# Summing the block products of a projection pair in three PSUM banks that are read between products

## The chip, the core and the metric

The kernel runs on one core of one Trainium2 chip. The metric is the device time of one execution in microseconds (us). An execution that the hardware profiler recorded is what the rows below come from. Engines go by the profile's names: PE (matmuls), PEld (weight loads, beside PE), DVE, ACT, POOL, and SP, whose queue issues the transfers.

## The reference, cut to what matters

One layer of a hybrid decoder trunk: 2048 tokens of 1024 channels are normalised, projected by one large matrix, sent through four mixers (RG-LRU, mLSTM, HGRN2, GLA), merged by gates, projected once more and normalised.

```python
def hybrid_mixer(h, w_in, ...):
    u = jnp.einsum('bsd,de->bse', h, w_in).astype(jnp.float32)
    (lru_x, lru_z, m_x, m_o, m_z, h_q, h_f, h_i, h_z,
     g_q, g_k, g_v, g_lr, g_z, merge) = jnp.split(u, idx, axis=-1)
...
    xa = causal_conv(lru_x, lru_conv_w, lru_conv_b)
    y_a = rg_lru(xa, lru_wa, lru_ba, lru_wx, lru_bx, lru_lambda) * jax.nn.silu(lru_z)
...
    gates = jax.nn.sigmoid(merge.reshape(B, S, N_BRANCH, D_MODEL))
    merged = jnp.sum(gates * proj, axis=2)
    return merged @ w_out
```

The change touches only the first line, the product `h @ w_in`, for the columns that are computed channel-major.

## The kernel before, in words

The tokens are worked on in two halves of 1024. In each half `ahead_pairs` (L459) computes 33 pairs of 128-column tiles of the projection with `ip_pair` (L400); then come the mixers and the merge, which the change leaves as they are.

A pair is a product of two blocks of tokens by two blocks of channels on one side, and two blocks of channels by two tiles of columns on the other. Eight block products would do it; `ip_pair` uses seven, in Winograd's form. The token side is split once per half (`split_first`, `split_blocks`: blocks `a11`, `a12`, `a22` and sums `s1` to `s4`). The weight side is made per pair: DVE forms four differences (`wsum`, L427) of the four loaded blocks `b11`, `b12`, `b22` (in the tiles `wr`) and `b21` (in a tile `gth`). For each product `product` (L411) splits its weight block in two float32r parts, the upper on ACT (L416, into a tile `wh`) and the rest on POOL (L417, into `wl`); there are six such buffers. Then PE runs 12 matmuls of 128x512 (L422): four channel blocks by three combinations of parts.

Each product has a PSUM bank of its own, the next of all eight in turn (`bank8`). The names `pb` and `mx` are those banks. The four result blocks are put together in SBUF: ACT copies the first product into `c11` (L437), and seven additions on DVE (`add`, L431) do the rest, each reading one bank and one or two SBUF blocks. `fin` then uses the pair: most take a tanh (L218) and a product (L477) or go to DRAM; those of `lru` run the RG-LRU of one channel tile, with convolutions (L704, L706), small matmuls (L735) and scans (L748) on DVE; those of `mx` run another convolution.

`GORD` (L42) fixes in which order pairs are written: one LRU pair, two path pairs, four times over, then the other paths and the gate pairs. What runs when on each engine is set by the scheduler of the framework, which orders all instructions by priorities and its own clock when the kernel is built. On the chip each engine takes its own queue in that fixed order.

Of the kernel before, what the change touches and what calls it, by code (L numbers as in the profile page):

```python
# [17 lines left out]
HT = 1024  # tokens of a half  # L18
DM = 1024
KT = 8  # k tiles of d_model  # L20
U = 516  # columns of one arena unit
NU = 16  # arena units that stay
NA = 4  # tiles of two units that are the arena's outside of the fast products
NY = 8  # the same, and branch outputs in the merge
NP = 6  # merge gates (of 32) computed between the mixers
NE = 5  # of these, so many for the first tokens while the others are split
EPS = 1e-6
NPB = 2  # PSUM banks of the input projection; the other ones are the mixers'
NG = 10  # arena units of the fast products; the other ones are what follows them
PRE = (("mx", 4), ("mo", 4), ("mz", 4), ("hq", 4), ("hz", 4), ("gz", 4), ("gq", 2), ("gk", 2))  # paths to DRAM, with their tiles  # L30
# [12 lines left out]
NORM = {"hz": "hnw", "gz": "gnw"}  # gate paths with the norm's weight in them  # L43
SILU = ("lz", "mz", "hq", "hz", "gz")
FILL = [0, 2, 0, 0, 0, 1, 0, 0, 1, 0, 0, 0, 2, 0]  # merge gates projected before each stage of the mixers

# columns of the packed per-channel vectors
# [10 lines left out]
# channel-major column tiles of the input projection, in the order of wc  # L58
# [10 lines left out]
# constants that depend on shapes alone  # L69
# [29 lines left out]
class Arena:  # L99
    """Units of U columns, handed out in program order, round and round; pairs start at even units."""  # L100
# [47 lines left out]
class Trunk:  # L148
# [107 lines left out]
    def proj_ch(self, pieces, rh, rl, sink, ns=(0, 1)):  # L256
        """128 columns of a product for 512 tokens at a time from weight pieces of 4 k tiles
        each: sink(token slice, PSUM [128, 512])."""
        nc = self.nc
# [22 lines left out]
    def ip_tok(self, pieces, ncol, evac, single=8):  # L282
        """Token-major column group: evac(first chunk, PSUM [128 tokens, chunks, ncol]); chunks one by one from some."""
        c0 = 0
        while c0 < 8:
            per = 512 // ncol if c0 < single else 1
            v = self.pbank()[:, 0:per * ncol].rearrange("p (c n) -> p c n", n=ncol)
            for cc in range(per):
                for k in range(KT):
                    self.tok_mm(v[:, cc, :], c0 + cc, k, pieces, ncol, k == 0, k == KT - 1)  # L290
            evac(c0, v)
            c0 += per

    def ip_tok_k(self, pieces, evac, ks):
        """The same for 256 columns, k outermost: the operands' tiles are done with one by one."""
# [13 lines left out]
    def split_first(self, xs):  # L309
        """The normalised input of the first tokens"""  # L310
# [7 lines left out]
    def load_first(self, xs):  # L318
        """The first tokens, and merge gates from them before the norm's factor is known"""
# [40 lines left out]
    def split_blocks(self, xs, st):  # L360
        """The other blocks (two of tokens by two of channels) that the products take: one more as it
        is, four sums; the block left out goes to DRAM."""
# [22 lines left out]
    def restore_block(self):  # L385
        """The block left out of the products, where its sum was."""
# [13 lines left out]
    def ip_pair(self, t0, t1, fin):  # L400
        """Two column tiles of 1024 tokens each; fin of both, [128, 3 free + 1024]."""
# [9 lines left out]
        def product(x, w):  # L411
# [6 lines left out]
            ps = self.bank8()  # L418
            for k, (xh, xl) in enumerate(self.op[x]):
                ws = slice(k * 128, (k + 1) * 128)  # L420
                for i, (wp, xp) in enumerate(((hi, xh), (hi, xl), (lo, xh))):
                    nc.tensor.matmul(ps, wp[:, ws], xp, start=(k == 0 and i == 0), stop=(k == 3 and i == 2))  # L422
            return ps
# [5 lines left out]
        def add(o, x, y):  # L429
            with self.prio(self.EV):  # L430
                V.tensor_tensor(o, x, y, op=ALU.add)  # L431
# [3 lines left out]
        p = product("a11", b11)  # L435
        with self.prio(self.EV):
            A.activation(c11, p, AF.Copy)  # L437
        wsum(b11, b12, b11)
        wsum(w2, b22, b11)
        p = product("s2", w2)  # L440
        add(c21, c11, p)
        p = product("s1", b11)
        add(c12, c21, p)
        wsum(b12, b22, b12)
        p = product("s4", b22)
        q = product("s3", b12)
        add(c22, c12, q)
        add(c21, c21, q)
        add(c12, c12, p)
        p = product("a12", b21)  # L450
        add(c11, c11, p)
        wsum(b21, b21, w2)
        p = product("a22", b21)
        add(c21, c21, p)
# [3 lines left out]
    def ahead_pairs(self):  # L458
        """The projections that the mixers take channel by channel, as far as no other channel or  # L459
        earlier token is needed, the RG-LRU, and merge gates: to DRAM."""  # L460
# [122 lines left out]
    def setup_mix(self):  # L583
        nc, c, a, col = self.nc, self.const, self.a, self.col
        V, A = nc.vector, nc.scalar
        # RG-LRU
# [8 lines left out]
        V.tensor_scalar(self.clru, self.clru, 4.0, None, op0=ALU.mult)  # 8 softplus(-lam) / 2  # L595
# [5 lines left out]
        # mLSTM: conv halved (for silu through tanh)  # L601
# [25 lines left out]
        # HGRN2 lower bound: cumulative softmax over the one layer, less its first  # L627
# [14 lines left out]
        # GLA  # L642
        nc.sync.dma_start(self.wlr, a["g_w_lr2"])

# [896 lines left out]
```

## Time and profile before

| | |
|---|---|
| median of 3 runs | 2736.16 us (2735.38 to 2738.37) |
| profiled execution, first to last instruction | 2737.5 us |
| what lies around that span | not told apart: the three runs end 2.1 us below to 0.9 us above it |
| busy | PE 95%, PEld 79%, DVE 63%, ACT 47%, POOL 55% |
| first half: pairs about 52 to 755 us, then mixers and merge | |
| second half: pairs about 1422 to 2111 us, then mixers and merge | |

A busy share is a mean over stages. PE's matmuls overlap, so the number of matmuls that a stretch starts tells more of its pace than the busy time does. The column PEclk is the granted share of the TensorE clock: 1.00 is 2.4 GHz, and a mean below it has some time at 1.2 GHz in it.

### The profile page before, as it was taken

The page shows a single profiled execution, that of the slowest core. Times are in us where ns is not written, and L with a number is a line of the kernel's source. Part 1 is how long each engine was busy: PE and PEld are TensorE (multiplying, and loading weights), DVE is VectorE, ACT ScalarE, POOL GpSimd, SP SyncE. Part 2 cuts the span into 40 slices and gives each one's busy share as a digit, 9 for nine tenths or more (in the row PEclk, how much of TensorE's full clock was granted, in tenths as well). Part 3 has the DMA queues.
Part 4 walks back from the last instruction along what each step waited for, and adds up shares of the span by engine and source line. Part 5 has one row for each costly group of instructions (what it writes and reads, how often), then busy time and mean ns, then how long its engine had stood idle before and what let it go on. Part 6 is the DMA issues. An engine that isn't in the chain of part 4 may idle for free. (4 is left out here: it accounts for less than half of the span.)

```text
span 2737.5 us, 45829 instructions
## 1 busy us (share of the span) xinstructions
PE 2603.8 (95%) x16800; PEld 2153.6 (79%) x16800; DVE 1736.1 (63%) x2907; ACT 1291.6 (47%) x2763; POOL 1499.7 (55%) x1273
## 2 busy tenths in 40 slices
PE   7889999999989898999999999999999999999999
PEld 5667788877878876778977777888787888777789
DVE  8987853346667767743478878533477677776332
ACT  5554554334444565542465545533344445644433
POOL 5556644444546545567476666444455556554753
PEclk9999999999999999999999999999999999989999
DMA  6132334243454435795442322433335533458821
GB/s 227 61 109 89 101 119 139 98 145 103 148 170 128 121 121 189 253 317 165 155 138 94 110 91 89 139 116 108 135 113 179 167 118 106 146 190 308 273 93 74
DMA packets 227072, 393.03 MB, mean 144 GB/s; under 512 B 20720, under 2 KB 78080, under 8 KB 226848
## 3 DMA queue, kind: packets, MB, share of 16 engines
q1 hardware_dynamic: 226848, 390.11, 42.7%
q8 instruction: 132, 2.16, 0.3%
q14 instruction: 92, 0.75, 0.1%
HBM read 270.42 MB, written 119.60 MB: 142 GB/s over the span
## 5 line engine op out<-in xcount | busy, mean ns | idle before, releaser
L417 POOL TENSOR_TENSOR wl<-wr,wh 128x512 fp32r<-128x512 f32 x264 | 371.6, 1411 | 302.4 <-ACT wh L416 294.4
L417 POOL TENSOR_TENSOR wl<-gth,wh 128x512 fp32r<-128x512 f32 x198 | 284.4, 1437 | 294.6 <-ACT wh L416 284.2
L422 PE MATMUL mx<-s,wh 128*128 128x512 f32 x1296 | 408.5, 395 | 11.3 <-DVE s L306 4.7
L431 DVE TENSOR_TENSOR arena<-arena,mx 128x512 f32<-128x512 f32 x348 | 229.4, 681 | 221.8 <-PE mx L422 208.5
L250 POOL TENSOR_TENSOR wl<-wr,wh 128x512 fp32r<-128x512 f32 (+1 forms) x176 | 250.4, 1431 | 175.4 <-ACT wh L249 139.8
L422 PE MATMUL mx<-hh,wh 128*128 128x512 f32 x760 | 302.0, 397 | 11.9 <-DVE arena L431 10.2
L422 PE MATMUL mx<-hh,wl 128*128 128x512 f32 x760 | 302.3, 398 | 3.1 <-POOL wl L417 3.1
L422 PE MATMUL mx<-hl,wh 128*128 128x512 f32 x760 | 302.0, 397 | 2.0 <-DVE hl L306 2.0
L422 PEld LDWEIGHTS mx<-s,wh 128*128 128x128 f32 x1296 | 243.9, 188 | 70.6 <-DVE s L306 7.1
L268 PE MATMUL pb<-hh,wh 128*128 128x512 f32 x704 | 286.9, 409 | 7.4 <-ACT hh L1284 2.6
L268 PE MATMUL pb<-hl,wh 128*128 128x512 f32 x704 | 286.5, 407 | 5.8 <-DVE hl L1285 5.8
L268 PE MATMUL pb<-hh,wl 128*128 128x512 f32 x704 | 284.3, 404 | 0.0
L416 ACT ACTIVATE wh<-wr 128x512 fp32r<-128x512 f32 x264 | 164.5, 627 | 232.7 <-PE mx L422 98.4
L280 PE MATMUL pb<-wh,hh 128*128 128x256 f32 (+1 forms) x880 | 254.2, 290 | 3.7 <-ACT arena L1006 1.5
L422 PE MATMUL mx<-s,wl 128*128 128x512 f32 x648 | 256.2, 396 | 0.9 <-POOL wl L417 0.9
L280 PE MATMUL pb<-wl,hh 128*128 128x256 f32 (+1 forms) x880 | 253.4, 288 | 1.7 <-POOL wl L250 1.7
L280 PE MATMUL pb<-wh,hl 128*128 128x256 f32 (+1 forms) x880 | 253.5, 288 | 0.0
L416 ACT ACTIVATE wh<-gth 128x512 fp32r<-128x512 f32 x198 | 124.4, 629 | 246.6 <-DVE gth L427 201.6
L249 ACT ACTIVATE wh<-wr 128x512 fp32r<-128x512 f32 (+1 forms) x176 | 110.0, 629 | 161.9 <-PE pb L268 106.6
L422 PEld LDWEIGHTS mx<-hh,wh 128*128 128x128 f32 x760 | 144.3, 190 | 50.1 <-ACT arena L218 11.0
L422 PEld LDWEIGHTS mx<-hh,wl 128*128 128x128 f32 x760 | 143.6, 189 | 41.0 <-POOL wl L417 8.2
L422 PEld LDWEIGHTS mx<-hl,wh 128*128 128x128 f32 x760 | 144.0, 189 | 38.1 <-DVE hl L306 3.2
(614 smaller groups left out, 6177.6 us busy)
## 6 DMA issues: line engine op xcount, KB each, us to landing
wr<-in_wc_dram SPq DMA_DIRECT2D x246, 256.0 KB, 2.7
g<-arena SPq DMA_DIRECT2D x52, 512.0 KB, 3.4
gth<-in_wc_dram SPq DMA_DIRECT2D x66, 256.0 KB, 2.8
wr<-in_wb_dram SPq DMA_DIRECT2D x64, 256.0 KB, 3.0
hl<-y SPq DMA_DIRECT2D x32, 512.0 KB, 5.9
arena<-g SPq DMA_DIRECT2D x48, 256.0 KB, 3.9
arena<-in_xT_dram SPq DMA_DIRECT2D x32, 256.0 KB, 5.1
lw<-g SPq DMA_DIRECT2D x32, 256.0 KB, 3.4
```

The source lines that it names most:

```text
L249: nc.scalar.activation(hi, raw, AF.Copy)
L250: nc.gpsimd.tensor_tensor(lo, raw, hi, op=ALU.subtract)
L268: nc.tensor.matmul(ps, w[:, ws], h[:, ts], start=(k == 0 and i == 0), stop=(k == nk - 1 and i == 2))
L280: self.nc.tensor.matmul(v, h[:, cs], w[:, ws], start=(first and i == 0), stop=(last and i == 2))
L416: A.activation(hi, w, AF.Copy)
L417: G.tensor_tensor(lo, w, hi, op=ALU.subtract)
L422: nc.tensor.matmul(ps, wp[:, ws], xp, start=(k == 0 and i == 0), stop=(k == 3 and i == 2))
L431: V.tensor_tensor(o, x, y, op=ALU.add)
```

## The change

A product no longer has a bank of its own. A pair takes three banks `p`, `q`, `r`. Bank `p` sums a11, then s2, then s3, then a22; bank `r` sums s1, then s4; bank `q` holds a12 alone. The matmuls of a later product start without clearing the bank, so they add to what is there. Between them the partial sums are read: `copy` (ACT) takes `c11`, `c12`, `c22` and `c21` out of a bank, and three additions on DVE are left, of `q` to `c11`, of `p` to `c22` and of `r` to `c12`. The product a12 moves from sixth place to second, and s3 goes ahead of s4.

The other lines of the diff take comments out. The lines below line 437 move down by three: `copy` is L435 in the changed kernel, the upper split L417, POOL's L418; additions stay L431 and matmuls L422; the LRU's matmuls are L738, its scans L751.

```diff
-        def product(x, w):
+        def product(x, w, ps, first=False):
...
-            ps = self.bank8()
             for k, (xh, xl) in enumerate(self.op[x]):
                 ws = slice(k * 128, (k + 1) * 128)
                 for i, (wp, xp) in enumerate(((hi, xh), (hi, xl), (lo, xh))):
-                    nc.tensor.matmul(ps, wp[:, ws], xp, start=(k == 0 and i == 0), stop=(k == 3 and i == 2))
-            return ps
+                    nc.tensor.matmul(ps, wp[:, ws], xp, start=(first and k == 0 and i == 0), stop=(k == 3 and i == 2),
+                                     skip_group_check=not first)
...
-        def add(o, x, y):
+        def add(o, ps):
             with self.prio(self.EV):
-                V.tensor_tensor(o, x, y, op=ALU.add)
+                V.tensor_tensor(o, o, ps, op=ALU.add)
+
+        def copy(o, ps):
+            with self.prio(self.EV):
+                A.activation(o, ps, AF.Copy)
...
-        p = product("a11", b11)
-        with self.prio(self.EV):
-            A.activation(c11, p, AF.Copy)
+        p, q, r = self.bank8(), self.bank8(), self.bank8()
+        product("a11", b11, p, True)
+        copy(c11, p)
+        product("a12", b21, q, True)
+        add(c11, q)
         wsum(b11, b12, b11)
         wsum(w2, b22, b11)
-        p = product("s2", w2)
-        add(c21, c11, p)
-        p = product("s1", b11)
-        add(c12, c21, p)
+        product("s2", w2, p)
+        copy(c12, p)
+        product("s1", b11, r, True)
+        copy(c22, r)
         wsum(b12, b22, b12)
-        p = product("s4", b22)
-        q = product("s3", b12)
-        add(c22, c12, q)
-        add(c21, c21, q)
-        add(c12, c12, p)
-        p = product("a12", b21)
-        add(c11, c11, p)
+        product("s3", b12, p)
+        add(c22, p)
+        product("s4", b22, r)
+        add(c12, r)
         wsum(b21, b21, w2)
-        p = product("a22", b21)
-        add(c21, c21, p)
+        product("a22", b21, p)
+        copy(c21, p)
```

The built order of the two kernels differs in three places that the prediction speaks of.

**DVE, gate pairs in the first half.** One pair of the kernel before: four weight differences (L427) and seven additions (L431).

```order
L427 TENSOR_TENSOR wr0_79<-wr1_80,wr0_79 128x512
L427 TENSOR_TENSOR gth1_95<-wr2_81,wr0_79 128x512
L427 TENSOR_TENSOR wr1_80<-wr2_81,wr1_80 128x512
L431 TENSOR_TENSOR arena_96<-arena_96,mx5_104 128x512
L431 TENSOR_TENSOR arena_96<-arena_96,pb1_98 128x512 x2
L431 TENSOR_TENSOR arena_96<-arena_96,pb0_97 128x512
L431 TENSOR_TENSOR arena_96<-arena_96,mx0_99 128x512
L431 TENSOR_TENSOR arena_96<-arena_96,mx1_100 128x512
L427 TENSOR_TENSOR gth0_94<-gth0_94,gth1_95 128x512
L431 TENSOR_TENSOR arena_96<-arena_96,mx3_102 128x512
```

The same of the change:

```order
L427 TENSOR_TENSOR wr0_79<-wr1_80,wr0_79 128x512
L427 TENSOR_TENSOR gth1_95<-wr2_81,wr0_79 128x512
L427 TENSOR_TENSOR wr1_80<-wr2_81,wr1_80 128x512
L427 TENSOR_TENSOR gth0_94<-gth0_94,gth1_95 128x512
L431 TENSOR_TENSOR arena_96<-arena_96,mx3_102 128x512
L431 TENSOR_TENSOR arena_96<-arena_96,mx5_104 128x512
L431 TENSOR_TENSOR arena_96<-arena_96,pb1_98 128x512
```

Four of the seven additions are gone, and the four differences stand together, since the operand of the last one is now used early.

**ACT, the same place of the change.** ACT's copies out of a bank (L435) stand between the weight splits (L417) of the same and the next pair.

```order
L417 ACTIVATE wh4_86<-wr2_81 128x512
L435 ACTIVATE arena_96<-mx5_104 128x512
L218 ACTIVATE arena_96<-arena_96 128x512 x2
L417 ACTIVATE wh1_83<-gth0_94 128x512
L435 ACTIVATE arena_96<-mx0_99 128x512
L435 ACTIVATE arena_96<-mx2_101 128x512
L417 ACTIVATE wh2_84<-gth1_95 128x512
L417 ACTIVATE wh0_82<-gth0_94 128x512
L435 ACTIVATE arena_96<-mx3_102 128x512
```

Before, one such row (L437) stood in each pair; now there are four, and each waits in one queue with splits that wait for a transfer or for a free buffer.

**PE, an LRU pair early in the first half.** The end of the product s2 in the kernel before, the product s1 and the start of the next one:

```order
L422 MATMUL mx1_100<-s0_3_582,wh5_87 128x512 x2
L422 MATMUL mx1_100<-s0_3_582,wl5_93 128x512
L422 MATMUL mx2_101<-s0_4_583,wh0_82 128x512 x2
L422 MATMUL mx2_101<-s0_4_583,wl0_88 128x512
L422 MATMUL mx2_101<-s0_5_584,wh0_82 128x512 x2
L422 MATMUL mx2_101<-s0_5_584,wl0_88 128x512
L422 MATMUL mx2_101<-s0_6_585,wh0_82 128x512 x2
L422 MATMUL mx2_101<-s0_6_585,wl0_88 128x512
L422 MATMUL mx2_101<-s0_7_586,wh0_82 128x512 x2
L422 MATMUL mx2_101<-s0_7_586,wl0_88 128x512
L422 MATMUL mx3_102<-s0_8_587,wh1_83 128x512 x2
```

Such a place of the change, where the third product of bank `p` (s3, of the operands `hh`) follows in the last row:

```order
L422 MATMUL mx1_100<-s0_3_582,wh0_82 128x512 x2
L422 MATMUL mx1_100<-s0_3_582,wl0_88 128x512
L422 MATMUL mx3_102<-s0_4_583,wh1_83 128x512 x2
L422 MATMUL mx3_102<-s0_4_583,wl1_89 128x512
L422 MATMUL mx3_102<-s0_5_584,wh1_83 128x512 x2
L422 MATMUL mx3_102<-s0_5_584,wl1_89 128x512
L422 MATMUL mx3_102<-s0_6_585,wh1_83 128x512 x2
L422 MATMUL mx3_102<-s0_6_585,wl1_89 128x512
L422 MATMUL mx3_102<-s0_7_586,wh1_83 128x512 x2
L422 MATMUL mx3_102<-s0_7_586,wl1_89 128x512
L738 MATMUL mx4_103<-wh0_82,wh5_87 128x512
L738 MATMUL mx5_104<-wh0_82,wh5_87 128x512
L422 MATMUL mx1_100<-hh0_63,wh2_84 128x512
```

Before, the bank `mx1` came up again only after seven products; now it is written again after one product and two small matmuls, and ACT's copy has to be through by then.

## Rows read from the trace of the kernel before

**Rows 1.** The page, busy time by engine over the span.

```profile
PE 2603.8 (95%) x16800; PEld 2153.6 (79%) x16800; DVE 1736.1 (63%) x2907; ACT 1291.6 (47%) x2763; POOL 1499.7 (55%) x1273
```

**Rows 2.** Busy time by stretch; the columns stand in the first line.

```profile
core 0: us, PE busy (x) PEld busy (x) DVE busy (x) ACT busy (x) POOL busy (x), PEclk, DMA share, GB/s
60.00:85.00 25.00, 15.49 (x59) 10.13 (x58) 25.00 (x35) 10.51 (x18) 16.83 (x11) 1.00 0.11 32
85.00:198.00 113.00, 99.28 (x392) 76.39 (x391) 102.75 (x130) 60.45 (x93) 64.63 (x43) 0.94 0.24 84
1440.00:1540.00 100.00, 87.34 (x354) 68.15 (x353) 89.12 (x113) 51.95 (x82) 56.62 (x39) 0.95 0.25 87
200.00:700.00 500.00, 499.17 (x2143) 396.52 (x2142) 290.08 (x396) 222.72 (x361) 259.59 (x193) 1.00 0.35 117
1600.00:2100.00 500.00, 499.42 (x2146) 397.22 (x2145) 296.52 (x404) 229.17 (x373) 261.61 (x191) 1.00 0.36 121
```

**Rows 3.** Whom PE waited for: 60 to 200 us, then 1400 to 1540 us.

```profile
PE mx L422 <- DVE arena L431: 6.8, 2, 5.1
PE pb L422 <- POOL wl L417: 3.3, 3, 1.7
...
PE mx L422 <- DVE arena L431: 6.4, 2, 5.1
```

**Rows 4.** Whom DVE waited for, 60 to 200 us.

```profile
DVE wr L427 <- DMA wr<-in_wc_dram: 6.0, 2, 3.9
DVE arena L737 <- ACT arena L218: 3.5, 2, 1.9
DVE arena L431 <- ACT arena L437: 0.5, 1, 0.5
```

**Rows 5.** Groups of the page: additions of two kinds of bank, ACT's copy.

```profile
L431 DVE TENSOR_TENSOR arena<-arena,mx 128x512 f32<-128x512 f32 x348 | 229.4, 681 | 221.8 <-PE mx L422 208.5
...
L431 DVE TENSOR_TENSOR arena<-arena,pb 128x512 f32<-128x512 f32 x114 | 75.6, 681 | 62.0 <-PE pb L422 61.5
L437 ACT ACTIVATE arena<-mx 128x512 f32<-128x512 f32 x52 | 30.3, 584 | 8.7 <-PE mx L422 6.4 <-DMA phf<-arena 2.2
```

**Rows 6.** Busy time of L431 alone by stretch (DVE busy, PEclk, DMA share, GB/s).

```profile
85.00:198.00 113.00, 22.13 (x34) 0.94 0.24 84
1440.00:1540.00 100.00, 19.69 (x30) 0.95 0.25 87
```

**Rows 7.** Timelines of PE, DVE and ACT among gate pairs: start, us, instruction.

```profile
1802.73 0.39 PE L422 MATMUL mx<-hl,wh 128*128 128x512 f32 x1
1802.96 0.39 PE L422 MATMUL mx<-hh,wl 128*128 128x512 f32 x1
1803.39 1.88 DVE L431 TENSOR_TENSOR arena<-arena,mx 128x512 f32<-128x512 f32 x3 [3.84 <-PE mx L422]
```

**Rows 8.** Whom ACT waited for, 85 to 198 us (total, times, longest).

```profile
ACT arena L218 <- DVE arena L706: 14.1, 5, 3.9
ACT arena L704 <- DVE arena L431: 12.6, 6, 5.0
ACT wh L416 <- DVE wr L427: 7.1, 2, 4.2
ACT wh L724 <- DVE arena L706: 5.0, 3, 2.9
ACT arena L218 <- DVE arena L431: 4.9, 4, 2.2
```

**Rows 9.** Whom ACT waited for, 200 to 700 us.

```profile
ACT wh L416 <- DVE gth L427: 86.4, 39, 5.4
```

**Rows 10.** Busy time by stretch, mixers of the first and of the second half.

```profile
800.00:1100.00 300.00, 274.60 (x2861) 239.43 (x2859) 219.64 (x496) 159.81 (x475) 165.52 (x176) 0.95 0.44 138
2200.00:2500.00 300.00, 279.94 (x3012) 239.04 (x3011) 228.57 (x498) 159.15 (x470) 163.31 (x174) 0.94 0.49 161
```

## The prediction

> **What bounds the kernel now.** Start with the busy shares [rows 1]: PE 95%, everything else far below. That says that only time in which PE is *not* at its pace can be won; it does not say where that time is. So the second view is busy time by stretch [rows 2]. In 200 to 700 us and in 1600 to 2100 us, where most pairs run, PE is busy 99.8% and starts 2143 and 2146 matmuls in 500 us: 4.29 per us, one every 0.233 us. There the pairs cannot go faster, whatever DVE does. In the first part of each half it is different. From 85 to 198 us PE starts 392 matmuls where 113 x 4.29 = 484 would fit, so 92 are missing, 21.5 us. From 1440 to 1540 us it is 354 of 429, so 75 are missing, 17.5 us; this is much the same work in the second half. In these two stretches DVE is busy 102.75 of 113 us and 89.12 of 100 us, ACT and POOL about half. The mean granted clock there is 0.94 and 0.95, so PE also spends some of that time at 1.2 GHz, after idling.
>
> Third view, the waits in these stretches. PE's longest waits there are for DVE's additions (L431: 6.8 us in two waits in the first, 6.4 us in the second), that is, for a bank that no one has read yet [rows 3]. DVE itself waits for 10.0 us in 140 [rows 4]. So DVE sets the pace from 85 to 198 us and, with more holes, from 1440 to 1540 us; PE sets it in the rest of the pair stages.
>
> **The change, part by part.** *Additions on DVE.* There are 66 pairs; 7 additions each are 348 + 114 = 462 [rows 5], and 3 each are 198. An addition takes 0.681 us [rows 5]; back to back three take 1.88 us, so one slot is 0.60 us [rows 7]. Over the kernel DVE loses 264 x 0.60 = 158 us of work. In the saturated stretches this is worth nothing, since PE is busy beside it. It counts only where DVE is late. From 85 us to 198 us the trace has 34 additions with 22.13 us [rows 6], 0.65 each. In the built order DVE has 33 additions ahead of its fourth LRU scan, which is where DVE's crowded stretch ends; the change has 13 ahead of the same scan. 20 x 0.65 = **13.0 us** less. By the order the second half is the same, 33 to 13, with 19.69 / 30 = 0.656 us each [rows 6]: **13.1 us**. So 26 us is the most that this term can give, and PE has room for it: 21.5 and 17.5 us are missing.
>
> How much of the 26 arrives? From below, zero: the path there may run through ACT's and POOL's work on the LRU, and DVE's share would only become idle time. From above, all of it: every slot that DVE drops lets the weight differences and convolutions behind it start sooner. The nearest row is the busy share of DVE, 91% and 89% [rows 2], which speaks for most of it; but PE waits for DVE's additions as such only 13 us in both stretches together, and the rest of its missing time is spread over late splits. I take 0.6, between the ends and above half for that busy share: **-15.6 us**.
>
> *Copies on ACT.* 198 more copies of 0.584 us [rows 5] are 116 us on ACT over the kernel, 5 points of share. In 85 to 198 us, with about 5 pairs, 15 copies add 9 us to 60.45 of 113 [rows 2]. ACT stays below DVE. Cost on the path: zero by amount. What they do to the order is the next item.
>
> *Reads between products.* 264 products now start in a bank that must have been read first: four of seven in a pair (s2, s3 and a22 in `p`, s4 in `r`). Three of these reads are ACT's copies, one is DVE's addition to `c22`. A read that is ready to go costs little: the last matmul of a product starts at 1802.96 and takes 0.39 us, the addition behind it starts at 1803.39, 0.04 us after its end [rows 7]; with 0.584 us for the copy that is 0.62 us. The cover is what PE has to do in between. Counted in the built order, with 0.233 us per matmul, the cover is under 2 us at 14 of the 264, under 3.6 us at 44, and 4.7 us or more, mostly two whole products, at 199. So in the saturated stretches a copy may be some 4 us late and cost nothing. ACT does wait there, 86.4 us in 39 waits, 2.2 us each, for the last weight difference alone [rows 9]; a copy queued behind one is still in time. Likely cost there: 0. Lower end 0, upper end in the second rival.
>
> A rule of the Trainium skill speaks against this part: "Perfetto Trace Analysis", section "Optimizing Tensor Performance", wants independent groups of matmuls to rotate through banks so that emptying one overlaps the next group. Its consequence for this kernel is the third rival; the sum itself goes by the cover in the built order.
>
> *Order of the products, transfers, POOL.* POOL's splits are the same 462. The same four loads are issued per pair by SP. The block `b21` is now needed second; its tile becomes free when the split of the pair before's a22 is through. Six split buffers let that happen up to five products ahead (5 x 12 x 0.233 = 14 us), more than a load and a split need, so I cost it at nothing. In return the last weight difference no longer waits for a late split, which takes away some of the waits in [rows 9]. If the lead is gone, as where DVE is late, the late load stands in ACT's queue ahead of copies, which is part of the second rival.
>
> *The mixers.* Their instructions are the same, but the scheduler has put them in a partly different order, because the additions ahead of them are gone. What such a shuffle is worth: the two halves do the same work in other orders, and PE's busy time in 300 us differs by 279.94 - 274.60 = 5.3 us [rows 10]. I take 0 for it, with about 6 us either way in the range.
>
> **Sum.** Against the profiled execution 2737.5 - 15.6 = 2721.9 us. The three runs lie around that span and their median is 1.3 us below it, so for the median 2736.16 - 15.6 = **2721 us** (2720.6).
>
> **Rivals.** *First: DVE is busy but does not set the pace.* The LRU's chain passes DVE, ACT and POOL in turn, and from 60 to 85 us DVE is full with the split of the token blocks [rows 2], which does not change. Then the 13 us become idle time on DVE, and the time is 2736 +/- 5. For it: in 85 to 198 us DVE has 10 us of idle time of its own. Against it: ACT waits for DVE, 43.7 us in 20 waits there [rows 8], and hardly the other way round. Chance 0.22.
>
> *Second, on the other side: late reads stop PE.* In the LRU pairs ACT's queue stands behind DVE's convolutions, waiting 2.2 us each time and 5.0 us at the longest [rows 8]. A copy behind such a wait comes 0.62 + 2.2 = 2.8 us after its product. Before, seven other banks were free; now PE stops at the 14 places with cover under 2 us (mostly 1.85 us): 14 x 1.0 = 13 us, and DVE's gain doesn't come, as PE and DVE wait for each other: 2736 + 13 = 2749 us. With the longest wait at each it is 14 x (5.6 - 1.85) = 53 us, 2789 us. It decides where ACT's copies are later than about 1.2 us at those places, or 4 us in the rest. For it: those short covers lie with the LRU pairs, where ACT waits most. Against it: DVE has less to do there, so ACT's waits should shrink. Chance 0.18.
>
> *Third: reads are not covered at all.* If each of the 264 products waited for its read in full, PE would stand still for 264 x 0.62 = 164 us: 2900 us. This is what the skill's rule on rotating banks would make of a single bank. The built order puts other banks' matmuls in between, so I give it 0.02.
>
> That the change does not do what it says is excluded by the order: 198 additions and 264 copies are there.
>
> **How the numbers follow.** A measurement of this kernel can tell about 0.2%, 5.5 us, from no change. The forecast of 2721 us has a chance of 0.56 and with its own ends (26 us and 6 us of shuffle below, some 6 us of gain above) spans 2704 to 2730. The first rival lies in 2731 to 2741, the second at 2749 and above. Range: from 2704, the bound of the gain with the shuffle, to 2748, which takes in the first rival and reaches to the second, and leaves out the rest of it. Faster 0.57 (forecast, and a little of the first rival's lower end), same 0.22, slower 0.21.
>
> **What would show it.** Right: in the windows 85 to 198 us and 1440 to 1540 us PE starts more matmuls (430 or more in the first, where there were 392), DVE's share there falls, the saturated stretches keep one matmul per 0.233 us and end some 8 us and 16 us earlier, and PE's wait for L431 is short. Wrong by the first rival: DVE's share falls and the number of matmuls does not rise. Wrong by the second: PE waits for ACT's copies (L435), or for DVE's additions, at the LRU pairs, and the granted clock in these stretches falls; if PE's share sinks below 99% in 200 to 700 us, the cover that I counted is not enough.

## The result, and the profile after

| | median us | runs | ratio to before |
|---|---|---|---|
| before | 2735.77 (2734.19 to 2738.37) | 4 | |
| the change | 2774.88 (2760.79 to 2789.59) | 4 | 1.0138 [1.0101, 1.0174] |

The change makes the kernel slower by 1.4%, 39 us. The forecast of 2721 us had the wrong sign, and the time lies above the range (2704 to 2748), on the side of the second rival. The profiled execution took 2760.79 us, its span is 2759.0 us; it is the shortest of the four.

Busy time by engine, from the page of the changed kernel (to be read against [rows 1]):

```profile
PE 2607.9 (95%) x16800; PEld 2144.8 (78%) x16800; DVE 1620.2 (59%) x2643; ACT 1402.6 (51%) x2973; POOL 1494.9 (54%) x1273
```

DVE lost 115.9 us and ACT got 111.0 us more: the work moved as the diff says. The same stretches as in [rows 2], with the same columns:

```profile
60.00:85.00 25.00, 15.40 (x50) 11.95 (x51) 25.00 (x36) 11.24 (x20) 15.52 (x10) 0.72 0.10 33
85.00:198.00 113.00, 101.98 (x415) 79.98 (x415) 97.55 (x115) 66.17 (x106) 66.25 (x46) 0.95 0.24 82
1440.00:1540.00 100.00, 88.31 (x359) 68.52 (x357) 81.80 (x99) 56.31 (x91) 53.50 (x38) 0.97 0.27 87
200.00:700.00 500.00, 495.02 (x2115) 390.53 (x2114) 240.22 (x289) 262.64 (x438) 256.05 (x188) 1.00 0.35 115
1600.00:2100.00 500.00, 494.82 (x2114) 390.31 (x2113) 244.39 (x294) 262.30 (x438) 254.40 (x186) 1.00 0.35 115
```

In the two crowded stretches PE starts 23 and 5 matmuls more (415 for 392, 359 for 354). In the two stretches that had been saturated it starts 28 and 32 fewer, 6.5 and 7.4 us at 0.233 us each. PE's waits from 50 to 200 us in the changed kernel (total, times, longest), to be read against [rows 3]:

```profile
PE mx L422 <- ACT s L305: 7.1, 1, 7.1
PE pb L422 <- DVE gv L628: 5.0, 1, 5.0
PE mx L422 <- ACT wh L417: 4.2, 1, 4.2
...
PE mx L422 <- ACT arena L435: 1.8, 1, 1.8
PE pb L422 <- DVE arena L431: 1.2, 1, 1.2
PE mx L422 <- DVE arena L431: 1.2, 1, 1.2
```

The waits for DVE's additions shrank from 6.8 us to 2.4 us. In their place PE waits for ACT: for the split of a token sum (L305), for a weight split (L417) and for a copy out of a bank (L435).

For the whole execution it helps to cut at the first and the last start of a pair matmul (L422) in each half. A **pair stage** lies between them; behind each comes a stage of mixers and merge. Busy time in these four stages, before (columns as in [rows 2]):

```profile
51.96:755.30 703.34, 679.28 (x2870) 536.07 (x2870) 462.61 (x625) 325.45 (x525) 377.73 (x275) 0.99 0.33 111
755.30:1422.40 667.10, 621.74 (x5523) 538.55 (x5521) 416.45 (x840) 321.32 (x858) 372.23 (x357) 0.97 0.54 177
1422.40:2111.76 689.36, 672.09 (x2861) 533.36 (x2860) 448.88 (x588) 324.52 (x526) 380.06 (x276) 0.99 0.34 116
2111.76:2737.50 625.74, 589.85 (x5386) 515.24 (x5384) 368.76 (x783) 290.24 (x798) 346.26 (x342) 0.96 0.50 165
```

The same for the changed kernel:

```profile
54.29:766.07 711.78, 684.26 (x2877) 540.18 (x2877) 409.23 (x498) 379.48 (x629) 378.20 (x274) 0.98 0.33 109
766.07:1422.86 656.79, 615.94 (x5516) 531.22 (x5514) 415.81 (x834) 323.59 (x861) 368.73 (x356) 0.98 0.55 180
1422.86:2132.94 710.08, 680.69 (x2860) 535.54 (x2861) 387.83 (x459) 376.40 (x626) 380.95 (x277) 0.99 0.34 111
2132.94:2759.00 626.06, 586.86 (x5385) 507.89 (x5383) 364.38 (x779) 293.22 (x802) 342.06 (x341) 0.98 0.51 166
```

Start-up +2.3, first pair stage +8.4, first mixers -10.3, second pair stage +20.7, second mixers +0.3: together +21.5 us, the difference of the two spans. So in these two profiles the loss is in the pair stages, **29.2 us**, where the forecast had a gain of 15.6 us.

### The profile page after: what moved, and what is told of

Its sections match the earlier page's. It is cut to its first block, busy times and chain, and to the rows that moved or that the text cites. A ratio compares the mean times of both kernels' runs of the same rounds, so it can differ in the third digit from the quotient of the medians.

```text
span 2759.0 us, 45452 instructions
## 1 busy us (share of the span) xinstructions
PE 2607.9 (95%) x16800; PEld 2144.8 (78%) x16800; DVE 1620.2 (59%) x2643; ACT 1402.6 (51%) x2973; POOL 1494.9 (54%) x1273
## 5 line engine op out<-in xcount | busy, mean ns | idle before, releaser
L418 POOL TENSOR_TENSOR wl<-wr,wh 128x512 fp32r<-128x512 f32 x264 | 364.2, 1388 | 378.3 <-ACT wh L417 303.0
L418 POOL TENSOR_TENSOR wl<-gth,wh 128x512 fp32r<-128x512 f32 x198 | 290.9, 1473 | 216.4 <-ACT wh L417 186.5
L422 PE MATMUL mx<-s,wh 128*128 128x512 f32 x1184 | 376.2, 396 | 17.2 <-ACT s L305 9.2
L422 PE MATMUL mx<-hh,wh 128*128 128x512 f32 x776 | 311.4, 402 | 23.8 <-ACT wh L417 9.7
L422 PE MATMUL mx<-hl,wh 128*128 128x512 f32 x776 | 310.7, 400 | 0.0
L422 PE MATMUL mx<-hh,wl 128*128 128x512 f32 x776 | 307.3, 400 | 2.9 <-POOL wl L418 2.9
L268 PE MATMUL pb<-hh,wh 128*128 128x512 f32 x704 | 286.2, 409 | 10.6 <-DVE gth L1314 3.9
L417 ACT ACTIVATE wh<-wr 128x512 fp32r<-128x512 f32 x264 | 164.3, 628 | 243.2 <-PE mx L422 131.6
L422 PEld LDWEIGHTS mx<-s,wh 128*128 128x128 f32 x1184 | 222.3, 189 | 77.3 <-ACT s L305 10.1
L280 PE MATMUL pb<-wh,hh 128*128 128x256 f32 (+1 forms) x880 | 252.5, 288 | 9.6 <-DVE lrt L1120 3.4
L280 PE MATMUL pb<-wl,hh 128*128 128x256 f32 (+1 forms) x880 | 253.1, 288 | 0.3 <-POOL wl L250 0.3
L280 PE MATMUL pb<-wh,hl 128*128 128x256 f32 (+1 forms) x880 | 252.5, 287 | 0.0
L431 DVE TENSOR_TENSOR arena<-arena,mx 128x512 f32<-128x512 f32 x148 | 100.8, 682 | 233.5 <-PE mx L422 167.9
L422 PE MATMUL mx<-s,wl 128*128 128x512 f32 x592 | 233.5, 396 | 0.0
L417 ACT ACTIVATE wh<-gth 128x512 fp32r<-128x512 f32 x198 | 124.7, 630 | 182.9 <-DVE gth L427 96.6
L422 PEld LDWEIGHTS mx<-hh,wh 128*128 128x128 f32 x776 | 148.8, 192 | 64.2 <-ACT wh L417 13.9
L249 ACT ACTIVATE wh<-wr 128x512 fp32r<-128x512 f32 (+1 forms) x176 | 110.7, 632 | 168.6 <-PE pb L268 77.8
L422 PEld LDWEIGHTS mx<-hh,wl 128*128 128x128 f32 x776 | 148.3, 191 | 40.5 <-POOL wl L418 4.2
L422 PEld LDWEIGHTS mx<-hl,wh 128*128 128x128 f32 x776 | 148.7, 192 | 37.3 <-issue 3.3
```

The lines of the kernel that those rows point to most:

```text
L249: nc.scalar.activation(hi, raw, AF.Copy)
L268: nc.tensor.matmul(ps, w[:, ws], h[:, ts], start=(k == 0 and i == 0), stop=(k == nk - 1 and i == 2))
L280: self.nc.tensor.matmul(v, h[:, cs], w[:, ws], start=(first and i == 0), stop=(last and i == 2))
L417: A.activation(hi, w, AF.Copy)
L418: G.tensor_tensor(lo, w, hi, op=ALU.subtract)
L422: nc.tensor.matmul(ps, wp[:, ws], xp, start=(first and k == 0 and i == 0), stop=(k == 3 and i == 2), skip_group_check=not first)
```

## The experiments

What was open: is DVE's relief worth nothing, or is it worth something and then lost? And lost to what: the reads between products, the moved product a12, ACT as the reader, or the shuffle of the mixers? The table gives the four stages of each kernel's profiled execution, cut as above, and the median of its timed runs against the runs of before on the same chip.

| kernel | pairs 1 | mixers 1 | pairs 2 | mixers 2 | median us | ratio |
|---|---|---|---|---|---|---|
| before | 703.3 | 667.1 | 689.4 | 625.7 | 2735.77 | |
| before_again | 703.5 | 661.0 | 689.1 | 625.9 | 2733.70 (one run) | |
| the change | 711.8 | 656.8 | 710.1 | 626.1 | 2774.88 | 1.0138 [1.0101, 1.0174] |
| again | 711.3 | 668.0 | 710.4 | 632.9 | 2778.09 | 1.0141 [1.0111, 1.0171] |
| own_banks | 698.5 | 663.9 | 688.3 | 634.4 | 2749.62 | 1.0045 [1.0023, 1.0067] |
| order_only | 705.2 | 675.4 | 691.8 | 639.7 | 2776.53 | 1.0133 [1.0105, 1.0161] |
| sums_only | 724.1 | 675.0 | 717.7 | 638.3 | 2807.47 | 1.0252 [1.0228, 1.0276] |
| copies_on_dve | 728.2 | 668.4 | 718.7 | 629.8 | 2811.70 | 1.0274 [1.0247, 1.0300] |
| sums_early | 705.9 | 679.5 | 696.6 | 642.8 | 2781.52 | 1.0155 [1.0130, 1.0179] |
| sums_late | 712.1 | 669.8 | 700.0 | 632.3 | 2767.84 | 1.0098 [1.0070, 1.0126] |
| not_first_three | 716.0 | 671.4 | 704.3 | 650.6 | 2794.88 | 1.0206 [1.0183, 1.0229] |
| sums_middle | 705.6 | 670.9 | 694.6 | 637.9 | 2766.31 | 1.0115 [1.0091, 1.0138] |
| one_shared | 717.9 | 651.9 | 706.3 | 627.8 | 2763.72 | 1.0102 [1.0080, 1.0124] |

**The same kernels once more.** No edit.

> The changed kernel once more, for a second profile. Its first four times differ by 1%, where the kernel before stays within 0.2%, and the profile taken was of the shortest. If the TensorE clock makes the difference, a longer run (about 2775 us) has some 30 to 60 us more at 1.2 GHz in its rows and the same waits in the same places; if waits make it, PE's idle time in the pair stages is longer than 32.5 and 31.5 us and the clock is as before.

> The kernel before, unchanged, once more with a profile. It tells how far the stages of one and the same program differ between executions. Theory (the pair stages cost what the change costs, the mixers' stages vary with the granted clock): the pair stages take 703 and 689 us as in the first profile, within 3 us each, while the mixers' stages may differ by up to 10 us from 667 and 626 us. Rival (the mixers' stages of the kernel before are always faster than those of the change): they lie within 3 us of 667 and 626 us.

The pair stages of one program come back within 0.5 us (703.3 and 703.5, 689.4 and 689.1; 711.8 and 711.3, 710.1 and 710.4). Those of mixers and merge do not: 11.2 and 6.8 us between the two executions of the changed kernel, 6.1 us in the first mixers of the kernel before. Mixers of the second execution of the change:

```profile
766.64:1434.68 668.04, 620.31 (x5516) 534.30 (x5514) 420.93 (x834) 323.12 (x860) 368.04 (x356) 0.98 0.55 177
...
2145.05:2777.93 632.88, 592.75 (x5385) 512.73 (x5383) 366.45 (x779) 293.12 (x802) 342.11 (x341) 0.97 0.51 164
```

The same matmuls keep PE busy 4.4 and 5.9 us longer than in the rows above, and PE stands 6.9 and 0.9 us longer. So neither reading of the longer run of the change named the place: of the 18.9 us by which its span is longer, 18.1 lie in the mixers and the merge. The mean granted clock, 0.982 and 0.978 over the two spans, makes some 23 us more at 1.2 GHz, less than the 30 to 60 expected; PE's idle time in the pair stages is 29.5 and 28.7 us, where it was 27.5 and 29.4, so the waits there do not make it. For the kernel before the theory held (pair stages within 3 us, mixers within 10) and the rival fell with the 6.1 us.

So a pair stage comes back sharply and a whole run does not; below, the pair stages are compared. They are not the whole price of an edit, since PE can get back behind a pair stage some of what it lost at its end (see the next experiment).

**Each product in its own bank.** The change as it is, but each product clears a bank of its own; all splits, copies, additions and the order in which the products are written stay.

```diff
-        product("s2", w2, p)
+        p = self.bank8()
+        product("s2", w2, p, True)
```

and so for s3, s4 and a22.

> The changed kernel, but each product starts in a cleared bank of its own (seven of the eight in turn), with the same copies, additions and order of products. The sums in the banks are left out, so c12, c21 and c22 lack terms. Theory of the late reads: PE no longer waits for a read between products, and the time falls below the kernel before, to about 2720 us, since DVE still has 264 additions less. Rival, the order of the products and ACT's longer queue: the waits for splits stay, and the time stays at 2760 to 2780 us.

Measured: 698.5 and 688.3 us, the shortest pair stages of all. The time did not fall to 2720 us, nor below the kernel before: 2749.62 us, 0.45% above it (interval 0.23% to 0.67%), though well below the change. The pair stages:

```profile
54.51:753.01 698.50, 677.30 (x2869) 537.69 (x2870) 406.04 (x494) 374.46 (x625) 375.82 (x270) 0.98 0.33 110
...
1416.90:2105.18 688.28, 671.62 (x2860) 531.77 (x2859) 388.58 (x459) 376.41 (x627) 380.77 (x274) 0.99 0.35 114
```

and the two saturated stretches of the same kernel:

```profile
200.00:700.00 500.00, 500.00 (x2156) 399.17 (x2155) 241.20 (x295) 265.32 (x444) 262.75 (x194) 1.00 0.36 118
1600.00:2100.00 500.00, 500.00 (x2156) 399.43 (x2155) 250.66 (x305) 266.53 (x447) 259.16 (x190) 1.00 0.37 122
```

With DVE's and ACT's work as in the change but a cleared bank for each product, PE is never idle there and starts 2156 matmuls; with shared banks it is 2115 and 2114. Over the pair stages the shared banks cost 13.3 and 21.8 us. Of this PE stands still for 6.3 and 12.7 us more (length less busy time: 27.5 against 21.2, 29.4 against 16.7). The other 7.0 and 9.1 us are busy time, for 8 matmuls more in the first half and none in the second; the slower clock is a part of that, see the end.

Not all of the 35.1 us stays lost. Behind each pair stage PE waits for a load of the mixers. In the 40 us from the last pair matmul on, own_banks first and the change second, first half and then second half:

```profile
PE mx L862 <- DMA ma<-pxm: 7.6, 2, 5.6
PE mx L862 <- DMA ma<-pxm: 8.2, 2, 5.8
...
PE mx L858 <- DMA ma<-pxm: 3.2, 2, 1.8
PE mx L858 <- DMA ma<-pxm: 2.5, 1, 2.5
```

The change waits 4.4 and 5.7 us less for this load, and over all of PE's waits in these 40 us 4.2 and 4.1 us less. So an estimated 8 to 10 us of the 35.1 come back and 25 to 27 stay. The ratios of the two kernels to the kernel before, 1.0138 and 1.0045, differ by some 25 us.

How much of it is PE waiting for a read is open. In the pair stages PE's waits that name an addition or a copy out of a bank come to 6.5 and 7.6 us in the change and 4.5 and 0.7 us in own_banks: 8.9 us more. The rows of the second pair stage, the change and then own_banks:

```profile
PE mx L422 <- DVE arena L431: 3.7, 4, 2.3
PE mx L422 <- ACT arena L435: 2.6, 1, 2.6
PE pb L422 <- DVE arena L431: 1.3, 1, 1.3
...
PE pb L422 <- DVE arena L431: 0.7, 1, 0.7
```

The other waits mostly name splits of tokens and weights, and the built order is not the same in the two kernels: in the last pair of the second half the change has a matmul of another product (L280) ahead of the pair's last products, and PE waits 3.1 us there for its weight split (L249). So the price is that of shared banks with the order that the scheduler gives them; the two are not told apart.

**The order of the products alone.** The kernel before, with a12 second and s3 ahead of s4.

```diff
         p = product("a11", b11)
         ...
+        q = product("a12", b21)
         wsum(b11, b12, b11)
         wsum(w2, b22, b11)
         ...
+        add(c11, c11, q)
         ...
-        p = product("s4", b22)
         q = product("s3", b12)
         ...
+        p = product("s4", b22)
         ...
-        p = product("a12", b21)
-        add(c11, c11, p)
```

> The kernel before with its seven banks and seven additions, but with the products in the order of the change (a12 second, s3 ahead of s4), the addition of a12 after c11 has been used. If the moved product costs (its block must be loaded and split right after the pair before's last one), the time rises by 10 us or more, to 2746 to 2775 us; if not, it stays within 5 us of 2736 us.

And the other way round: the change, with a12 back in sixth place.

```diff
-        product("a12", b21, q, True)
-        add(c11, q)
         ...
         product("s4", b22, r)
         add(c12, r)
+        product("a12", b21, q, True)
+        add(c11, q)
```

> The change without its move of a12: sums in banks, copies and three additions, but a12 in sixth place, so that s2 follows a11 in the same bank directly. If it is the reads between products that cost, this is worse than the change, since one product less lies between them: pair stages of 715 us and more, 2785 us or above. If the moved product were the cost, it would come back to 2736 to 2745 us.

The new order (a12 second, s3 ahead of s4) costs 1.9 and 2.4 us in the pair stages of the kernel before. The median of order_only, 2776.53 us, is above all that the expectation named, and the pair stages do not explain that. Together with the sums the move of a12 helps: without it the pair stages take 724.1 and 717.7 us and the whole 2807.47 us, as expected if the reads cost. Between order_only and own_banks the written order is the same and DVE's additions go down from seven to three: 6.7 and 3.5 us less. That is what the relief of DVE gives, with ACT's added copies in it. New order and relief together, from the kernel before to own_banks, make the pair stages only 4.8 and 1.1 us shorter. The fourth LRU scan, where DVE's crowded stretch ends, shows how that comes about. It starts so many us after the first pair matmul of its half:

| | before | order_only | own_banks | the change |
|---|---|---|---|---|
| fourth scan, first / second half | 144.2 / 130.6 | 148.5 / 135.5 | 138.7 / 130.1 | 139.3 / 133.0 |

Against order_only the 20 additions less bring it forward by 9.8 and 5.4 us; against the kernel before by 5.5 and 0.5 us. order_only takes 1.3% more in all, and most of that is in the mixers, whose instructions nothing touched, though the scheduler orders them otherwise there too:

```profile
758.42:1433.79 675.37, 627.22 (x5523) 543.60 (x5521) 417.06 (x841) 319.87 (x859) 373.36 (x360) 0.95 0.54 176
2125.61:2765.31 639.70, 592.83 (x5386) 515.19 (x5384) 370.62 (x785) 292.17 (x803) 347.71 (x345) 0.96 0.50 164
```

**DVE as the reader.** The change, with the copies out of the banks on DVE.

```diff
-                A.activation(o, ps, AF.Copy)
+                V.tensor_copy(o, ps)
```

> The changed kernel with its four copies per pair on DVE in place of ACT. If ACT's queue makes the reads and splits late, the time falls to 2740 us or below, though DVE has its seven bank reads per pair back; if the reads between products as such cost, DVE being the more crowded engine in the LRU pairs makes it worse: 2780 us or more.

The pair stages are 16.4 and 8.6 us longer than in the change. PE's waits from 50 to 200 us:

```profile
PE mx L422 <- DVE arena L435: 14.2, 5, 10.7
PE pb L422 <- DVE arena L435: 4.4, 2, 3.1
```

The second branch of the expectation held (2811.70 us): PE waits 18.6 us for DVE's copies in this stretch, where in the change it waited 1.8 us for ACT's.

**Where the sums cost.** `np` counts the pairs of a half; `old()` is the form before, seven banks and seven additions.

```diff
+        self.np += 1
+        if self.np > 12:
+            old()
+        else:
             p, q, r = self.bank8(), self.bank8(), self.bank8()
```

In sums_early the condition is `self.np > 12`, in sums_late `self.np <= 12`, in not_first_three `self.np <= 3`, in sums_middle `not 12 < self.np <= 28`.

> The first 12 pairs of each half (the four LRU pairs and the path pairs between them) sum in banks as in the change; the other 21 have the seven banks and seven additions of the kernel before. Theory now: the sums cost where operands and reads come late, that is while the token blocks are still being split and in the LRU pairs. Then the two pair stages stay some 8 and 20 us longer than before (711 and 710 us) and the time stays near 2770 us. Rival, the cost lies in all pairs alike: 12 of 33 of it, 3 and 7 us, and about 2747 us.

> The reverse: the first 12 pairs of each half as in the kernel before, the other 21 summed in banks. If the cost lies in the first pairs, the pair stages are within 3 us of 703 and 689 us and the time is near 2740 us. If it lies in all alike, 21 of 33 of it stays: 708 and 702 us, and about 2755 us.

> Only the first three pairs of each half as in the kernel before, the other 30 summed in banks. It tells the start, where token blocks are still being split and the sums forbid PE to take whatever product is ready, from the LRU pairs behind it. If the start is the cause, the wait of 7 us for ACT's split of s1 is gone and the pair stages fall to about 703 and 695 us; if the reads in the LRU pairs are, they stay at 708 us or more.

> Pairs 13 to 28 of each half are summed in banks as in the change, the other 17 (the first twelve with all LRU pairs, and the last five) as before. Theory (the reads between products cost only where a half begins, in the LRU pairs, and at the end of the pair stage): the pair stages take at most 4 us longer than before, 703 to 707 and 689 to 693 us, and DVE still loses 16 x 4 additions per half, which are worth nothing there. Rival (every summed pair costs some): about half of what the change cost, 708 and 700 us.

Early sums cost 2.6 and 7.2 us in the pair stages, late ones 8.8 and 10.6. So the theory that the cost lies in the first pairs fell twice: early sums did not keep all of it, and late sums are not within 3 us of the kernel before. The stages are nearer to the rivals' numbers (3 and 7 us; 708 and 702 us), but the cost is not alike in all pairs either, as the table below shows. Leaving the first three pairs as before doesn't help: 716.0 us in the first half is more than with all pairs summed, and 704.3 us in the second lies between the two branches; why was not tried further. For sums_middle the theory holds in the first half (705.6, at most 707 expected) and is missed by 1.6 us in the second (694.6). One wait for a read is seen there, in PE's waits from 200 to 700 us:

```profile
PE mx L422 <- ACT arena L435: 1.9, 1, 1.9
```

It stands at the first summed pair, and the second half has one of 2.4 us at the same place. To see where the rest lies, each pair stage is cut in five: the time until PE had started so many pairs' worth (84 each) of its L422 matmuls. First half / second half, us:

| pairs' worth | before | own_banks | the change | one_shared | sums_middle |
|---|---|---|---|---|---|
| 0 to 4 | 112.5 / 99.6 | 110.1 / 97.4 | 113.6 / 105.7 | 112.6 / 99.6 | 112.6 / 100.1 |
| 4 to 12 | 171.0 / 170.0 | 169.9 / 172.4 | 172.4 / 174.3 | 175.3 / 174.1 | 170.7 / 171.3 |
| 12 to 22 | 194.7 / 194.6 | 194.5 / 194.6 | 194.7 / 194.6 | 194.6 / 194.6 | 196.8 / 197.6 |
| 22 to 32 | 205.9 / 206.0 | 204.8 / 204.7 | 208.3 / 208.4 | 208.6 / 210.3 | 206.3 / 206.4 |
| 32 to 33 | 19.2 / 19.2 | 19.2 / 19.2 | 22.8 / 27.1 | 26.8 / 27.7 | 19.2 / 19.2 |

In the middle, where all pairs are alike, ten pairs take 194.5 to 194.7 us in these kernels, but for the first summed pair of sums_middle: reads between products cost nothing there. They cost where other work lies among that of the pairs. The change less own_banks is 6.0 and 10.2 us in the first twelve pairs with the LRU, 3.5 and 3.7 us from pair 22 on, where some 40 matmuls of other lines stand between those of the pairs, and 3.6 and 7.9 us at the last pair, where the mixers' work begins. PE's waits for a read in the change stand among the first twelve pairs and in the last one. From pair 22 to 32 it has none: PE waits there 1.4 and 1.5 us, for weight splits, where own_banks waits for nothing, so how the sums cost there is not shown.

**One shared bank.** The kernel before, with a22 summed onto s3: six additions, one read between products. The order is not quite that of the kernel before: s3 is moved ahead of s4, so that s4 and a12 stand between s3 and a22.

```diff
-        p = product("s4", b22)
         q = product("s3", b12)
         add(c22, c12, q)
-        add(c21, c21, q)
+        p = product("s4", b22)
         ...
-        p = product("a22", b21)
-        add(c21, c21, p)
+        product("a22", b21, q)
+        add3(c21, c21, q)
```

`product` takes the bank as in the change; `add3` is `add` of the kernel before, written `add` in the lines above that it shares.

> The kernel before, in its order of products, with only s3 and a22 summed in one bank: six additions instead of seven, and one read between products per pair, with a12's product between. Theory: one product of a pair that must wait for a read, with another product as cover, costs at the few places of the LRU pairs and the end only: pair stages within 5 us of before (703 and 689 us), and the 66 additions that go are worth about 1 us. Rival (any read between products costs like the change's): a quarter of 13 and 22 us above the stages with banks of their own, 703 to 707 and 694 us. The total may move by 10 us with the mixers' order in either case.

Both expectations fell: the pair stages are 14.6 and 16.9 us longer. PE's waits from 680 to 770 us in this kernel:

```profile
PE mx L422 <- DVE arena L441: 5.9, 2, 5.4
PE pb L422 <- DVE arena L441: 2.9, 1, 2.9
```

In the kernel before PE waited for none of the pairs' reads near that place (700 to 770 us); it waited for a load of the mixers, just after the pairs:

```profile
PE mx L880 <- DMA ma<-pxm: 6.5, 1, 6.5
```

Over the pair stages of one_shared PE's waits for L441 come to 13.2 and 18.7 us, where those for L431 in the kernel before were 6.8 and 6.4. So one read between products per pair, on DVE and behind a chain of additions, is enough for such a loss, with two products as cover; what the moved s3 costs by itself was not tried. Some comes back: behind the later end of the pairs the mixers take 651.9 us instead of 667.1 and 661.0.

**One such wait, instruction by instruction.** In an LRU pair of the second half, the changed kernel has this built order on ACT:

```
L435 ACTIVATE arena_96<-mx1_100 128x512
L707 ACTIVATE arena_96<-arena_96,hmc_192 128x512
L218 ACTIVATE arena_96<-arena_96 128x512 x2
L435 ACTIVATE arena_96<-mx4_103 128x512
L435 ACTIVATE arena_96<-pb0_97 128x512
```

The bank `mx4` holds s2, whose last matmul started at 1511.88 us and took 0.40; s1 runs in `pb0` as cover; then s3 goes into `mx4`. Timeline of the changed kernel (start, duration, engine, instruction, idle time and releaser):

```profile
1512.70 3.79 DVE L709 SCALAR_TENSOR_TENSOR arena<-arena,hmc 128x512 f32<-128x512 f32 x4
...
1514.65 0.40 PE L422 MATMUL pb<-s,wl 128*128 128x512 f32 x1
1515.86 1.29 ACT L218 ACTIVATE arena<-arena 128x512 f32<-128x512 f32 x2 [2.15 <-DVE arena L709]
...
1517.06 0.58 ACT L435 ACTIVATE arena<-mx 128x512 f32<-128x512 f32 x1
...
1517.69 0.79 PE L422 MATMUL mx<-hh,wh 128*128 128x512 f32 x1 [2.64 <-ACT arena L435]
```

The tanh (L218) ahead of the copy waits 2.15 us for DVE's convolution (L709). The copy is ready to go at 1512.28 us and ends at 1517.64, 5.4 us later, where the product in between gives 12 x 0.233 = 2.8 us of cover. PE stops for 2.64 us.

## Why the prediction was wrong, point by point

*What bounds the kernel.* Right as far as it went: PE is at its pace in the middle (own_banks starts 13 and 10 matmuls more there, 3.0 and 2.3 us), and PE waited for DVE in the crowded stretches. With fewer additions PE's waits for L431 there fall from 6.8 to 2.4 us.

*"How much of the 26 arrives?"* The direction was right, the size was not: 6.7 + 3.5 = 10.2 us (order_only to own_banks) where 0.6 x 26 = 15.6 us was taken. The factor is 0.39, if all of it belongs to that term. At the fourth scan it is 9.8 + 5.4 = 15.2 us, close to what was taken, but a third of that is gone again by the end of the pair stages. PE's waits for DVE's additions, 13 us in both stretches, were the nearer row. And the relief needs the new order, with which only 4.8 + 1.1 = 5.9 us against the kernel before are left.

*"Copies on ACT ... cost on the path: zero by amount."* Not refuted: in own_banks ACT carries the same copies, and the pair stages are the shortest of all.

*"Reads between products ... Likely cost there: 0."* **This is the step that failed.** Sharing the banks costs 13.3 + 21.8 = 35.1 us in the pair stages (own_banks), of which an estimated 8 to 10 come back behind them. The cover was counted rightly where pairs are alike (194.6 us per ten pairs with or without shared banks), and at most of the places that is so. But I measured how late a read is by its duration and by the gate pairs of [rows 7]. In the LRU pairs and at the last pair the reader's queue holds work that waits for another engine, and one read in an LRU pair came 5.4 us after its product. With a bank for each product such a read stops PE less often; now the next product into that bank waits for it. That is shown at such places and, with DVE as the reader, in one_shared and copies_on_dve; for the rest of the 35.1 us, where PE's waits name splits or nothing, it is argued. The rule that I weighed there speaks of it: the Trainium skill, "Perfetto Trace Analysis", section "Optimizing Tensor Performance", would have independent groups rotate through banks. The trace agrees in the sign, and own_banks prices the rotation at 35.1 us of the pair stages here; in the middle of them it is worth nothing.

*"Order of the products, transfers, POOL ... I cost it at nothing."* The moved a12, with s3 ahead of s4, costs 1.9 + 2.4 = 4.3 us in the kernel before (order_only). Term by term the pair stages come to 4.3 - 10.2 + 35.1 = 29.2 us. That this meets the measured sum proves nothing, as the terms are differences along one row of kernels; each is built in an order of its own, and the terms carry that too.

*The mixers, "0 for it, with about 6 us either way".* Too narrow. With the same instructions the first mixers took 651.9 to 679.5 us and the second 625.7 to 650.6 us over these kernels, and one program differs by up to 11.2 us from run to run. Of the 39.1 us between the medians, 29.2 are the pair stages, 2.3 to 3.4 the start-up, and some 7 are left for the mixers and the merge, where the two profiles of the change give -10.0 and +8.1. That this is no small matter shows in order_only: it is as slow as the change in all, with pair stages only 4.3 us longer than before. What order there is better, and why, stays open.

*The rivals.* The second named the mechanism, the place, the engine and the signs: waits for L435 and L431, fewer matmuls in 200 to 700 us. PE's share there is 99.0%, just at the mark that the prediction had set. The measured 39 us lie between its 13 us and its 53 us with the longest waits. Its places were only in part the right ones: the 14 of short cover lie in the first eleven pairs of the halves, so the last pair and the stretch from pair 22 on were not among them, and the slower clock behind a wait was not in it. The first rival cannot be dismissed: the crowded stretch of the first half gained matmuls in the change, 415 for 392, but own_banks, which has the relief without the sharing, starts 396 and 354 in the two stretches, where the kernel before starts 392 and 354:

```profile
85.00:198.00 113.00, 98.43 (x396) 75.99 (x396) 99.65 (x112) 65.96 (x106) 65.43 (x45) 0.94 0.24 84
1440.00:1540.00 100.00, 88.06 (x354) 66.82 (x353) 84.00 (x97) 59.17 (x96) 58.63 (x39) 0.95 0.26 87
```

Without the sharing, then, the change would have come close to what that rival said. The third fell: 164 us were expected of uncovered reads.

## What to carry to other kernels

A product that adds to a bank which someone reads in between can put the reader's whole queue on PE's path; so ask how late the read can be at its worst place, behind the longest wait in that queue, and not how long a read takes. Cover counted in the steady part says nothing of the first and last pairs. And before paying for fewer additions, try them with banks of their own: here own_banks, which leaves the sums out, has pair stages 5.9 us shorter than the kernel before (10.2 us shorter than with seven additions in the same order) and is no faster in all, so there was little to pay for. No version here beat the kernel before.

## What the runs showed that was not expected

PE's clock falls behind a wait. In the changed kernel around the wait above (columns as in [rows 2]):

```profile
1510.00:1514.60 4.60, 4.60 (x21) 3.74 (x20) 4.50 (x7) 3.68 (x7) 2.44 (x2) 1.00 0.81 275
1517.70:1521.10 3.40, 3.40 (x8) 2.72 (x9) 2.05 (x4) 0.43 (x1) 0.00 (x0) 0.50 0.41 155
1521.10:1524.00 2.90, 2.90 (x14) 2.36 (x14) 1.53 (x3) 1.86 (x3) 0.43 (x1) 1.00 0.01 5
```

The granted clock is 1.00 (2.4 GHz) before the wait, 0.50 (1.2 GHz) in the 3.4 us after it, then 1.00 again: 8 matmuls start where 14.6 would. So behind this wait of 2.64 us PE does some 1.5 us less work (6.6 x 0.233). By the clock records of the traces the pair stages of the change have 29.8 and 20.5 us at 1.2 GHz, those of own_banks 23.2 and 10.2; at half the pace that is an estimated 3.3 and 5.2 us of the busy time that the shared banks add, 7.0 and 9.1 us. Where PE does not set the pace a slower clock need not cost: before_again has PE busy 3.1 us longer in the first pair stage than the first profile of the same kernel (682.40 for 679.28), and the stage is 0.2 us longer:

```profile
52.19:755.72 703.53, 682.40 (x2869) 538.84 (x2870) 462.12 (x624) 325.30 (x525) 377.71 (x275) 0.98 0.34 110
```

That the clock falls because of the wait was not tried.

And a single run says little of this program: the changed kernel spreads over 29 us (2760.79 to 2789.59), and its profile lies at the low end; the kernel before spreads over 4 us in the same four runs, but over 18 us (2733.29 to 2751.11) in 13 later runs.
